# Transposes of a head issued by turns with the values of the head ahead of it, and the next stage's first weights handled ahead of a layer norm

## The chip, the cores and the metric

One core of one Trainium2 chip. The metric is the device time of one execution in microseconds (us); the kernel before has a median of 1176.0 us over three runs (1175.67 to 1176.55). Engines are called by their names or as the profile does: TensorE is PE, VectorE is DVE, ScalarE is ACT, GpSimd is POOL, SyncE is SP.

## The reference, cut to what matters

Two decoder layers over 512 positions of width 1024 in float32; each layer is a token mixer, an output projection, a layer norm, a convolutional feed-forward block and a second layer norm. The change lies in the mixer of layer 0 (16 attention heads of width 64) and at the layer norms.

```python
# layer 0: 8 heads with a learned selection of keys (a), 8 heads with a forgetting gate (b)
la = einsum('bthr,btkr->bhtk', ql, c_sel) + bias;  pa = softmax(la);  oa = einsum('bhtk,btkr->bthr', pa, c_sel)
lb = einsum('bthd,bshd->bhts', qb, k_b) + gate;    pb = softmax(lb);  ob = einsum('bhts,bshd->bthd', pb, v_b)
mix = concatenate([oa, ob]) @ w_o
x = layer_norm(ALPHA * x + mix)          # then conv_ffn and a norm; layer 1: gated MLP and short conv, norm, conv_ffn, norm
```

## The kernel before

Every product of float32 matrices is made of three reduced-precision products: both operands are split into a high and a low part, and `mms` (L183) or `mm3` (L177) issues high x high, high x low, low x high into one PSUM bank. A weight block arrives by DMA in a `raw` tile of 128 x 1024 (three of them), ACT casts the high part (L77) and DVE or POOL subtracts for the low part (L81, L79); `Stream.get` keeps two blocks split ahead of use, and a `raw` tile is free for the next load when its low part is made.

The attention of layer 0 goes head by head, 0 to 15. The 512 queries are four chunks j of 128, and causal masking leaves chunk j with 128 (j+1) keys. For a head:

- **logits** (L628): 12 products with 64-row operands, in four groups of three (128, 256, 384 and 512 columns wide), into three banks.
- **soft** (L648): for each chunk DVE adds the bias and takes the minimum (L655), and ACT takes the exponential with its sum (L657) into a tile `d`.
- **turn** (L669): ten transposes of 128 x 128 through PE (L675) bring `d` into the one `tri` area of PSUM, keys first. An odd head adds a transpose of the reciprocal sums (L678) with a small copy on ACT (L680). Then `cut2` (L227) splits all 1280 columns into `pt`: a cast on ACT (L230), then a subtraction on DVE (L231).
- **values** (L689): 12 products of `pt` with the values, 512, 384, 256 and 128 columns wide. Their stationary operand has 64 columns for an even head and 128 for an odd one. ACT copies the result out (L713).
- **divide** (L721), once for two heads: a product, a cast (L727) and a subtraction (L728).

The string `SEQ` sets in what order these are issued for the heads. It is gone through once for each h from 0 to 19: L is logits(h), B the bias of h+1, T is turn(h-1), S is soft(h), D is divide(h/2-2), V is values(h-2), and a digit is that many **fill products**, taken from the projections of later heads, which need nothing of these stages. In turn, `fill(1)` also stands after each transpose. From about head 11 on no fill products are left until the output projection's are let in at head 15. I call a stage of a head by its letter and the head's number: T11 are the transposes of head 11.

Written order is not the order that the engines get: a scheduler sorts the instructions of each engine by its own model of time, and each engine runs its list in order. So the order of each engine, and not the code alone, tells what a change moves.

A layer norm (`out_ln`, L288) works on four chunks n of 128 rows while the last products of the stage ahead run: DVE adds and takes statistics (L259 to L263), POOL raises to -0.5 (L264), DVE and ACT scale (L267, L270), POOL adds (L271), and PE transposes the chunk into the next stage's operand (L282, 4 at a time, two halves of a chunk). In its loop it lets one weight block be split ahead with each chunk: `ws.ready(base[0] + n + 1)`. There are four norms; the second one (between the feed-forward of layer 0 and layer 1) is the place called "the second norm" below. The first weight blocks of layer 1 are two held in `quad` tiles and then blocks in `whi`/`wlo` tiles. One block of layer 1 passes a mask on POOL ahead of its split (`mask_w`, an affine select, L817).

Of the kernel before, what the change touches and what calls it, by code (L numbers as in the profile page):

```python
# [18 lines left out]
NCH = 4  # L19
# [6 lines left out]
EPS = 1e-5  # L26
BIG = 1e30
TAIL = 4
SEQ = "L4BT2SDV3"
POOL_CUT = range(12, 23)  # L30
S1, S2, S3, S4 = 4, 3, 1, 2
WARM, WARM2 = 7, 5
# [63 lines left out]
def _body(ctx, tc, A):  # L96
# [23 lines left out]
    def quad(dt=FR):  # L120
        return quads.tile([128, 4, 512], dt, name="quad")

    ws = Stream(nc, A["ws"], rawp, wp, 2)
# [65 lines left out]
    def both(*runs):  # L189

        runs = list(runs)
        while runs:
            for r in list(runs):
                if next(r, "end") == "end":
                    runs.remove(r)

    def xk(xt, k, a=0, b=S):
        return xt[0][k // 4][:, k % 4, a:b], xt[1][k // 4][:, k % 4, a:b]
# [39 lines left out]
    def load_gb(l, i):  # L238
        q = quad(F32)
        for s, src in enumerate((A["ln_g"], A["ln_b"])):  # L240
            nc.gpsimd.dma_start(q[:, 2 * s:2 * s + 2].rearrange("p a b -> p (a b)"),
                                src[l, i].partition_broadcast(128))
        return [q[:, j] for j in range(4)]
# [44 lines left out]
    def out_ln(lhs, nk, res_src, l, i, dst, nbig, last=False, begun=None):  # L288

        head = nk - TAIL  # L290
        if begun is None:
            pb = [[None, None] for _ in range(NCH)]
            for hf in range(2):
                for n in range(NCH):
                    pb[n][hf] = bank()
            for k in range(head, nk + (0 if last else nbig)):
                ws.big[base[0] + k] = quad

            for k in range(head):
                w = unit()  # L300
                for hf in range(2):
                    for n in range(NCH):
                        mm3(pb[n][hf], lhs(k, n), wk(w, hf * 512, hf * 512 + 512), k == 0, False)
        else:
            pb, run = begun
            for _ in run:
                pass
        us = [unit() for _ in range(TAIL)]
        gb = load_gb(l, i)
        xt = None if last else [[quad(), quad()], [quad(), quad()]]  # L310
        rs = []
        for n in range(NCH):
            rs.append(load_res(res_src, n))
            for hf in range(2):
                for k in range(head, nk):
                    m = mm3(pb[n][hf], lhs(k, n), wk(us[k - head], hf * 512, hf * 512 + 512),
                            k == 0, k == nk - 1)
                if not last and hf == 0 and n >= 2:
                    ln_turn(n - 2, rs[n - 2], xt, m)
            ln_chunk(n, pb[n], rs[n], gb, dst)  # L320
            if not last:
                ws.ready(base[0] + n + 1)
        late = None if last else [lambda m, n=n: ln_turn(n, rs[n], xt, m) for n in (2, 3)]
        return xt, late
# [54 lines left out]
    with ExitStack() as m0:  # L379
# [248 lines left out]
        def logits(h):  # L628

            q = made[h // 2]  # L630
            d = biases.pop(h)
            r = slice(64 * (h % 2), 64 * (h % 2) + 64)
            b01, b2, b3 = bank(), bank(), bank()
            lg = [b01[:, :128], b01[:, 128:384], b2[:, :384], b3]

            def run(j):
                n = 128 * (j + 1)
                c = slice(j * 128, j * 128 + 128)
                return mms(lg[j], (q[r, 0, c], q[r, 1, c]), (q[r, 2, :n], q[r, 3, :n]), True, True)

            both(run(0), run(2))
            both(run(1), run(3))
            st_[h] = (d, lg)

        rd_d = dr.tile([8, 2 * NCH, 128], F32, name="rd_d")
# [23 lines left out]
        def turn(h):  # L669
            d = st_[h][0]  # L670
            p = tri.tile([128, 1536], F32, name="tri")
            for i in range(NCH):
                for j in range(i, NCH):
                    o = PO[i] + (j - i) * 128
                    nc.tensor.transpose(p[:, o:o + 128], d[:, OFF[j] + i * 128:OFF[j] + i * 128 + 128], ident)  # L675
                    fill(1)
            if h % 2 == 1:
                nc.tensor.transpose(p[:8, 1280:1408], rds.pop(h // 2), ident)  # L678
                row = temp()[:8, :128]
                nc.scalar.copy(row, p[:8, 1280:1408])  # L680
                nc.scalar.dma_start(rd_d[h // 2], row)
            pt = ptp.tile([128, 2, 1280], FR, name="pt")
            cut2(pt[:, 0], pt[:, 1], p[:, :1280])
            st_[h] = pt

        oq = []
# [2 lines left out]
        def values(h):  # L689
            pt = st_.pop(h)  # L690
            if h % 4 == 0:
                oq.append(quad())
            i = h // 2
            v = vB if h < 8 else vA
            b0 = 64 * (h % 2)
            r = slice(b0, b0 + 64)
            p = bank()
            m = b0 + 64
            hv = h % 8
            if h % 2 == 0:  # L700
                ot[i] = [temp()]
            t = ot[i][0]

            def run(k):
                f = slice(64 * hv - b0, 64 * hv + 64)
                c = slice(PO[k], PO[k] + 512 - 128 * k)
                return mms(p[:m, k * 128:], (v[0][:, k, f], v[1][:, k, f]), (pt[:, 0, c], pt[:, 1, c]),
                           k == 0, k == 2)

            both(run(0), run(3))  # L710
            both(run(1))
            both(run(2))
            nc.scalar.copy(t[r], p[r])  # L713
            if h % 2 == 1:
                rb = temp()
                for e in range(2):
                    nc.sync.dma_start(rb[64 * e:64 * e + 64], rd_d[i, 4 * e:4 * e + 4].rearrange(
                        "a b -> (a b)").partition_broadcast(64))
                ot[i].append(rb)
# [48 lines left out]
        for h in range(20):  # L768
            for c in SEQ:
                if c == "L" and h < 16:  # L770
                    while h // 2 not in finished and next(todo, "end") != "end":
                        pass
                    logits(h)
                    if h == 15:
                        for _ in todo:
                            pass
                        todo = begun
                elif c == "B":
                    bias(h + 1)
                elif c == "D" and h >= 4 and h % 2 == 0:  # L780
                    divide(h // 2 - 2)
                elif c == "S" and h < 16:
                    soft(h)
                    step(S3)
                    soft2(h)
                    step(S4)
                elif c == "T" and 1 <= h <= 16:
                    turn(h - 1)
                elif c == "V" and 2 <= h <= 17:
                    values(h - 2)  # L790
                elif c.isdigit():
                    fill(int(c))
        ps3.close()
# [185 lines left out]
```

## Time and profile before

| | |
|---|---|
| median of three runs | 1176.0 us (1175.67 to 1176.55) |
| the profiled execution, its own time | 1176.91 us |
| its span on the core | 1175.2 us, of 14440 instructions |
| mean granted clock of PE | 0.995 of full speed |
| PE busy | 1160.9 us, 99% |
| DVE, ACT, POOL busy | 59%, 40%, 16% |

The span is the profiler's window on the core, 1.7 us shorter than the time of the same execution. The heads from 11 on, which have no fill products between their stages, lie at 194 to 222 us; the second norm lies at 620 to 650 us. A busy PE is a PE that has work; whether that work is at full clock is told by the granted clock of the stretch (1.00 is the 2.4 GHz level, 0.50 the 1.2 GHz level).

### The profile page before, as it was taken

What the parts mean: (1) busy time and instruction counts of PE and PEld (TensorE: products, weight loads), DVE (VectorE), ACT (ScalarE), POOL (GpSimd) and SP (SyncE); (2) the same over time, 40 slices, a digit from 0 to 9 for tenths busy, and PEclk for the clock granted to TensorE, in tenths of its full rate; (3) what the DMA queues carried; (4) which work ended last, traced back from release to release, by engine and by line L of the source; (5) the groups of instructions that cost most, each with busy time, mean ns of one, the idle gap of its engine ahead of it and who ended that gap; (6) DMA issues with size and microseconds to landing.
All of it is one profiled execution on the core that took longest, in us unless ns stands there. A gap on an engine that the chain in (4) does not pass through costs nothing. (4 is left out here: it accounts for less than half of the span.)

```text
span 1175.2 us, 14440 instructions
## 1 busy us (share of the span) xinstructions
PE 1160.9 (99%) x5532; PEld 967.0 (82%) x5532; DVE 697.9 (59%) x1137; ACT 464.5 (40%) x701; POOL 185.5 (16%) x242
## 2 busy tenths in 40 slices
PE   9999999999999999999999999999999999999997
PEld 7887878789888888888888888889888888888885
DVE  6799975657656666552237854465665565652226
ACT  7625656623444443432234243332544434432121
POOL 1319645314000000010004200012000000010003
PEclk9999999899999999999999999999999999999999
DMA  7623202353232322343353234371223223344221
GB/s 245 228 73 103 60 32 69 99 161 126 76 104 90 106 92 92 124 141 127 108 164 112 75 108 129 125 239 64 90 90 105 92 93 104 108 144 143 92 88 72
DMA packets 41381, 132.03 MB, mean 112 GB/s; under 512 B 5448, under 2 KB 5520, under 8 KB 41312
## 3 DMA queue, kind: packets, MB, share of 16 engines
q1 hardware_dynamic: 36128, 115.36, 30.3%
q0 software_dynamic: 5056, 15.71, 4.2%
q8 instruction: 43, 0.70, 0.3%
q14 instruction: 26, 0.21, 0.1%
q10 hardware_dynamic: 128, 0.03, 0.0%
HBM read 122.63 MB, written 10.02 MB: 113 GB/s over the span
## 5 line engine op out<-in xcount | busy, mean ns | idle before, releaser
L81 DVE TENSOR_TENSOR wlo<-raw,whi 128x1024 fp32r<-128x1024 f32 x150 | 185.2, 1235 | 273.1 <-ACT whi L77 272.9
L179 PE MATMUL bank<-quad,whi 128*128 128x512 f32 (+2 forms) x860 | 325.5, 380 | 0.4 <-ACT whi L144 0.4
L180 PE MATMUL bank<-quad,whi 128*128 128x512 f32 (+2 forms) x860 | 325.3, 378 | 0.0
L181 PE MATMUL bank<-quad,wlo 128*128 128x512 f32 (+2 forms) x860 | 325.2, 378 | 0.0
L77 ACT CAST whi<-raw 128x1024 fp32r<-128x1024 f32 x158 | 166.2, 1053 | 238.1 <-PE bank L181 107.3
L179 PEld LDWEIGHTS bank<-quad,whi 128*128 128x128 f32 x860 | 161.7, 188 | 31.2 <-ACT whi L144 1.5
L181 PEld LDWEIGHTS bank<-quad,wlo 128*128 128x128 f32 x860 | 161.7, 188 | 29.7
L180 PEld LDWEIGHTS bank<-quad,whi 128*128 128x128 f32 x860 | 161.7, 188 | 29.2
L180 PE MATMUL bank<-wlo,quad 128*128 128x512 f32 x356 | 138.5, 389 | 0.0
L181 PE MATMUL bank<-whi,quad 128*128 128x512 f32 x356 | 138.3, 389 | 0.0
L179 PE MATMUL bank<-whi,quad 128*128 128x512 f32 x356 | 138.0, 389 | 0.0
L249 POOL DMA_DIRECT2D temp<-x x24 | 13.2, 548 | 566.8 <-ACT quadx L365 424.4
L180 PEld LDWEIGHTS bank<-wlo,quad 128*128 128x128 f32 x356 | 66.8, 188 | 14.0
L181 PEld LDWEIGHTS bank<-whi,quad 128*128 128x128 f32 x356 | 66.8, 188 | 14.0
L179 PEld LDWEIGHTS bank<-whi,quad 128*128 128x128 f32 x356 | 66.8, 188 | 13.6
L334 DVE SCALAR_TENSOR_TENSOR temp<-bank,fcw,temp 128x511 f32<-128x511 f32 x88 | 65.5, 744 | 9.1 <-ACT temp L333 9.1
L180 PE MATMUL bank<-quad 128*128 128x512 f32 (+1 forms) x192 | 68.5, 358 | 0.6 <-DVE quad L81 0.6
L179 PE MATMUL bank<-quad 128*128 128x512 f32 (+1 forms) x192 | 67.8, 357 | 0.5 <-ACT quad L230 0.5
L181 PE MATMUL bank<-quad 128*128 128x512 f32 (+1 forms) x192 | 67.9, 356 | 0.0
L336 DVE SCALAR_TENSOR_TENSOR temp<-bank,fcw,temp 128x510 f32<-128x510 f32 x88 | 65.9, 748 | 3.0
L333 ACT ACTIVATE temp<-bank,fcw 128x512 f32<-128x512 f32 x88 | 60.0, 682 | 10.8 <-PE bank L181 10.8
L361 ACT ACTIVATE temp<-temp 128x512 f32<-128x512 f32 x44 | 27.8, 632 | 89.0 <-DVE temp L336 89.0
(164 smaller groups left out, 1479.3 us busy)
## 6 DMA issues: line engine op xcount, KB each, us to landing
raw<-in_ws_dram SPq DMA_DIRECT2D x190, 512.0 KB, 3.5
x<-temp SPq DMA_DIRECT2D x24, 256.0 KB, 2.0
temp<-x POOLq DMA_DIRECT2D x24, 256.0 KB, 3.2
temp<-in_xT_dram SPq DMA_DIRECT2D x8, 256.0 KB, 6.7
temp<-fk_d SPq DMA_DIRECT2D x8, 256.0 KB, 3.8
temp<-rd_d SPq DMA_DIRECT2D x16, 128.0 KB, 3.8
temp<-in_x_dram POOLq DMA_DIRECT2D x8, 256.0 KB, 3.5
quad<-in_ln_g_dram POOLq DMA_DIRECT2D x4, 512.0 KB, 4.9
```

Of the source, the lines that this page charges most:

```text
L77: nc.scalar.copy(hi, t)
L81: dve[0] = nc.vector.tensor_tensor(out=lo, in0=t, in1=_f(hi), op=ALU.subtract)
L179: nc.tensor.matmul(out, a[0], b[0], start=first, stop=False)
L180: nc.tensor.matmul(out, a[0], b[1], start=False, stop=False)
L181: return nc.tensor.matmul(out, a[1], b[0], start=False, stop=last)
L249: nc.gpsimd.dma_start(t, src[n * 128:n * 128 + 128, hf * 512:hf * 512 + 512])
L333: nc.scalar.mul(t, p, cw[:, j, 2:3])
L334: nc.vector.scalar_tensor_tensor(out=t[:, 1:], in0=p[:, :S - 1], scalar=cw[:, j, 1:2], in1=t[:, 1:], op0=ALU.mult, op1=ALU.add)
L336: nc.vector.scalar_tensor_tensor(out=t[:, 2:], in0=p[:, :S - 2], scalar=cw[:, j, 0:1], in1=t[:, 2:], op0=ALU.mult, op1=ALU.add)
L361: nc.scalar.activation(tg, tg, AF.Silu)
```

## The change

1. `SEQ` goes from "L4BT2SDV3" to "L7BX5SD7". X takes the products of turn(h-1) and of values(h-2) **by turns**, a transpose and then a product, until one of them is out. The fill products in T are gone; a head has 19 of them before (4 + 10 + 2 + 3) and after (7 + 5 + 7).
2. The transposes go by chunks of queries (`JS`): all that needs chunk 0 first, then chunk 1, and so on; before, they went by chunks of keys.
3. For heads 12 to 15 the split of `pt` comes in two pieces, of 512 and 768 columns.
4. In values, the products of 384 columns are no longer mixed with the rest: first 512 and 128 by turns as before, then 384, then 256 (in a generator that X can take from).
5. `out_ln` calls `ws.ready` for two blocks more than the next stage's `quad` blocks ahead of the norm's loop, when it is not the last norm.

The code from L196 on moves down by 2 to 8 lines: L230 becomes L233, L675 becomes L682, L186 becomes L187, L77 and L81 become L78 and L82.

```diff
-SEQ = "L4BT2SDV3"
+SEQ = "L7BX5SD7"
+JS = (0, 1, 2, 3)
...
         us = [unit() for _ in range(TAIL)]
         gb = load_gb(l, i)
+        if not last:
+            ws.ready(base[0] + nbig + 2)
...
-            for i in range(NCH):
-                for j in range(i, NCH):
+            for j in JS:
+                for i in range(j + 1):
                     o = PO[i] + (j - i) * 128
                     nc.tensor.transpose(p[:, o:o + 128], d[:, OFF[j] + i * 128:OFF[j] + i * 128 + 128], ident)
-                    fill(1)
+                    yield
...
-            cut2(pt[:, 0], pt[:, 1], p[:, :1280])
+            for c in ((slice(0, 1280),) if h < 12 else (slice(0, 512), slice(512, 1280))):
+                cut2(pt[:, 0, c], pt[:, 1, c], p[:, c])
...
-            both(run(0), run(3))
-            both(run(1))
-            both(run(2))
+            yield from both(run(0), run(3))
+            yield from run(1)
+            yield from run(2)
...
-                elif c == "T" and 1 <= h <= 16:
-                    turn(h - 1)
-                elif c == "V" and 2 <= h <= 17:
-                    values(h - 2)
+                elif c == "X":
+                    for _ in both(*([turn(h - 1)] if 1 <= h <= 16 else []),
+                                  *([values(h - 2)] if 2 <= h <= 17 else [])):
+                        pass
```

**The last heads on ACT.** The list of ACT in the kernel before, from the cast of head 10's `pt` (`pt_2149`) to that of head 11's (`pt_2217`); `d_2128` is head 12, and the three casts to `quad` are weight blocks of the output projection.

```order
L230 CAST pt_2149<-tri_2135 128x1280
L713 COPY temp_2092<-bank_2163 64x512
L657 ACTIVATE d_2128,den_2221<-d_2128,mn_2220 128x384
L727 CAST quad_2090<-temp_2092 128x512
L77 CAST quad_2408<-raw_2406 128x1024
L77 CAST quad_2413<-raw_2411 128x1024
L77 CAST quad_2418<-raw_2416 128x1024
L657 ACTIVATE d_2128,den_2221<-d_2128,mn_2220 128x128
L657 ACTIVATE d_2128,den_2221<-d_2128,mn_2220 128x256
L680 COPY temp_2214<-tri_2202 8x128
L230 CAST pt_2217<-tri_2202 128x1280
```

The same stretch after; `d_2131` is head 12, `d_2195` head 13, `pt_2229` is the probabilities of head 11 (those of head 10 stand 4 rows ahead of the first row).

```order
L664 ACTIVATE d_2131,den_2236<-d_2131,mn_2235 128x256
L664 ACTIVATE d_2131,den_2236<-d_2131,mn_2235 128x384
L664 ACTIVATE d_2131,den_2236<-d_2131,mn_2235 128x512
L735 CAST quad_2060<-temp_2062 128x512
L78 CAST quad_2412<-raw_2410 128x1024
L78 CAST quad_2417<-raw_2415 128x1024
L78 CAST quad_2422<-raw_2420 128x1024
L664 ACTIVATE d_2195,den_2306<-d_2195,mn_2305 128x128
L664 ACTIVATE d_2195,den_2306<-d_2195,mn_2305 128x256
L664 ACTIVATE d_2195,den_2306<-d_2195,mn_2305 128x384
L687 COPY temp_2226<-tri_2202 8x128
L233 CAST pt_2229<-tri_2202 128x1280
```

Between the cast for head 10 and that for head 11 there now stand all four exponentials of head 12 and three of head 13; before, three of head 12 and none of head 13.

**The same heads on PE.** The kernel before, from the last products of V10's first group: `bank_2235` is V10, `bank_2250` to `bank_2252` L13, `tri_2202` T11, `bank_2297` V11.

```order
L186 MATMUL bank_2235<-pt_2149,quad_1552 64x128
L186 MATMUL bank_2250<-quad_1863 128x128 x3
L186 MATMUL bank_2250<-quad_1863 128x256 x3
L675 MATMUL tri_2202<-ident_137,d_2038 128x128 x10
L678 MATMUL tri_2202<-ident_137,rd_2085 8x128
L186 MATMUL bank_2235<-pt_2149,quad_1552 64x512
```

And after, the same work; `bank_2204` is V10, `bank_2250` and `bank_2251` L13, `tri_2202` T11.

```order
L187 MATMUL bank_2204<-pt_2160,quad_1521 64x128
L187 MATMUL bank_2250<-quad_1846 128x128 x3
L187 MATMUL bank_2250<-quad_1846 128x256 x3
L187 MATMUL bank_2251<-quad_1846 128x384 x3
L682 MATMUL tri_2202<-ident_137,d_2051 128x128 x3
L187 MATMUL bank_2204<-pt_2160,quad_1521 64x512
L682 MATMUL tri_2202<-ident_137,d_2051 128x128
L187 MATMUL bank_2204<-pt_2160,quad_1521 64x128
L682 MATMUL tri_2202<-ident_137,d_2051 128x128
L187 MATMUL bank_2204<-pt_2160,quad_1522 64x512
L682 MATMUL tri_2202<-ident_137,d_2051 128x128
L187 MATMUL bank_2204<-pt_2160,quad_1522 64x128
```

The ten transposes of T11 stood in a row; now three do, and a product of V10 follows each of the rest. V11 follows in both kernels when V10 and L13 are done, and T12 is by turns with V11 in the same way.

**The second norm on DVE and POOL.** The list of DVE before: the first row is the last of the feed-forward's blocks, `wlo_5454` and `wlo_5460` are later blocks of layer 1, `temp_5214` is the norm's chunk 0.

```order
L81 TENSOR_TENSOR quad_5204<-raw_5202,quad_5204 128x1024
L81 TENSOR_TENSOR wlo_5454<-raw_5451,whi_5453 128x1024
L259 SCALAR_TENSOR_TENSOR temp_5214<-temp_5214,bank_4641 128x512
L261 BN_STATS st_5242<-temp_5214 128x6
L259 SCALAR_TENSOR_TENSOR temp_5216<-temp_5216,bank_4645 128x512
L81 TENSOR_TENSOR wlo_5460<-raw_5457,whi_5459 128x1024
L261 BN_STATS st_5242<-temp_5216 128x6
```

The first two blocks of layer 1 come some 25 rows later, in the middle of the norm's last chunk (`temp_5374`):

```order
L259 SCALAR_TENSOR_TENSOR temp_5374<-temp_5374,bank_4644 128x512
L81 TENSOR_TENSOR quad_5371<-raw_5369,quad_5371 128x1024
L81 TENSOR_TENSOR quad_5435<-raw_5433,quad_5435 128x1024
L261 BN_STATS st_5416<-temp_5374 128x6
L259 SCALAR_TENSOR_TENSOR temp_5376<-temp_5376,bank_4648 128x512
```

After, all of them stand ahead of chunk 0 (`temp_5244`), with `wlo_5740` behind its first row:

```order
L82 TENSOR_TENSOR quad_5212<-raw_5210,quad_5212 128x1024
L82 TENSOR_TENSOR quad_5220<-raw_5218,quad_5220 128x1024
L82 TENSOR_TENSOR quad_5225<-raw_5223,quad_5225 128x1024
L82 TENSOR_TENSOR wlo_5231<-raw_5228,whi_5230 128x1024
L82 TENSOR_TENSOR wlo_5237<-raw_5234,whi_5236 128x1024
L262 SCALAR_TENSOR_TENSOR temp_5244<-temp_5244,bank_4649 128x512
L82 TENSOR_TENSOR wlo_5740<-raw_5737,whi_5739 128x1024
L264 BN_STATS st_5272<-temp_5244 128x6
L262 SCALAR_TENSOR_TENSOR temp_5246<-temp_5246,bank_4653 128x512
```

On POOL, the mask stood behind three chunks of the norm; after, it stands ahead of the first chunk's power (L267, L264 before):

```order
L244 DMA quad_5215<-in_ln_b_dram 128x1024
L825 AFFINE_SELECT raw_5749<-raw_5749 128x1024
L267 TENSOR_TENSOR rs_5275<-ve_5274,mhalf_140 128x1
L274 TENSOR_TENSOR temp_5244<-temp_5244,quad_5215 128x512
L274 TENSOR_TENSOR temp_5246<-temp_5246,quad_5215 128x512
```

The two `quad` blocks and the two after them are now split in the order in which they are loaded, and the mask of a later block is on POOL ahead of the norm.

## Rows read from the trace of the kernel before

**Rows 1.** Busy time of each engine, share of the span, instructions (the page).

```profile
PE 1160.9 (99%) x5532; PEld 967.0 (82%) x5532; DVE 697.9 (59%) x1137; ACT 464.5 (40%) x701; POOL 185.5 (16%) x242
```

**Rows 2.** Stretches: length, busy time of PE, PEld, DVE, ACT, POOL; clock; DMA share, GB/s.

```profile
100.00:194.00 94.00, 94.00 (x510) 74.74 (x509) 74.42 (x189) 59.09 (x130) 59.23 (x93) 1.00 0.23 71
194.00:222.00 28.00, 26.40 (x148) 21.89 (x146) 21.15 (x54) 21.24 (x51) 14.14 (x20) 0.88 0.29 87
...
630.00:660.00 30.00, 29.40 (x144) 23.91 (x144) 27.73 (x62) 13.19 (x20) 17.09 (x15) 1.00 0.40 142
```

**Rows 3.** PE's timeline in the last heads: start, length, line, operation, [idle before <- releaser].

```profile
201.30 2.19 PE L186 MATMUL bank<-quad 64*128 64x128 f32 x12
...
209.99 0.56 PE L186 MATMUL bank<-pt,quad 128*128 128x512 f32 x2 [0.96 <-ACT pt L230]
...
213.65 2.37 PE L675 MATMUL tri<-ident,d 128*128 128x128 f32 x10 [0.63 <-DVE rd L665]
215.66 3.60 PE L186 MATMUL bank<-pt,quad 128*128 128x512 f32 x12
219.19 2.17 PE L186 MATMUL bank<-quad 64*128 64x128 f32 x12
```

**Rows 4.** Finer stretches of the last heads, columns as in rows 2.

```profile
212.00:214.00 2.00, 1.37 (x6) 0.82 (x5) 2.00 (x6) 1.32 (x5) 0.45 (x1) 0.53 0.78 236
...
218.00:220.00 2.00, 2.00 (x12) 1.73 (x12) 1.45 (x2) 0.58 (x1) 1.34 (x3) 0.77 0.00 0
```

**Rows 5.** PE's paces in the heads before: fill products, transposes and values.

```profile
156.88 0.48 PE L186 MATMUL bank<-quad 128*128 128x512 f32 x1
...
157.22 0.48 PE L186 MATMUL bank<-quad 128*128 128x512 f32 x1
...
161.21 2.07 PE L186 MATMUL bank<-pt,quad 128*128 128x512 f32 x12
163.12 0.39 PE L186 MATMUL bank<-quad,whi 128*128 128x512 f32 x1
...
180.05 1.25 PE L675 MATMUL tri<-ident,d 128*128 128x128 f32 x10
181.06 0.48 PE L186 MATMUL bank<-quad,whi 128*128 128x512 f32 x1
```

**Rows 6.** ACT's timeline in the last heads.

```profile
204.72 2.95 ACT L77 CAST quad<-raw 128x1024 fp32r<-128x1024 f32 x3
207.56 0.40 ACT L657 ACTIVATE d<-d,mn 128x128 f32<-128x128 f32 x1
...
208.73 1.21 ACT L230 CAST pt<-tri 128x1280 fp32r<-128x1280 f32 x1
```

**Rows 7.** DVE's timeline in the last heads.

```profile
201.59 1.49 DVE L231 TENSOR_TENSOR pt<-tri,pt 128x1280 fp32r<-128x1280 f32 x1 [0.42 <-ACT pt L230]
203.00 0.55 DVE L655 CUSTOM_DVE_ANT_0 d<-bank,d 128x384 f32<-128x384 f32 x1
```

**Rows 8.** The second norm: PE, ACT and POOL timelines, and the mask's line.

```profile
636.40 0.60 PE L282 MATMUL bank<-ident,temp 128*128 128x128 f32 x4
...
646.30 0.40 PE L181 MATMUL bank<-quad 128*128 128x512 f32 x1
646.53 0.39 PE L179 MATMUL bank<-quad 128*128 128x512 f32 x1
647.47 0.50 PE L180 MATMUL bank<-quad 128*128 128x512 f32 x1 [0.55 <-DVE quad L81]
...
631.50 1.05 ACT L77 CAST whi<-raw 128x1024 fp32r<-128x1024 f32 x1 [4.87 <-DMA raw<-in_ws_dram]
...
629.95 0.99 POOL L264 TENSOR_TENSOR rs<-ve,mhalf 128x1 f32<-128x1 f32 x1 [75.22 <-DVE ve L263]
633.25 2.97 POOL L271 TENSOR_TENSOR temp<-temp,quad 128x512 f32<-128x512 f32 x2 [2.31 <-ACT temp L270]
...
L817 POOL TENSOR_SCALAR_AFFINE_SELECT raw<-raw x1: 1100/1100/1100, 650.3 to 650.3; 128x1024 f32<-128x1024 f32 x1
```

More of the change, by code (lines that the diff above doesn't have):

```diff
@@ L195, in both @@
                     runs.remove(r)
+                else:
+                    yield
     def xk(xt, k, a=0, b=S):
@@ L639, in run @@
                 return mms(lg[j], (q[r, 0, c], q[r, 1, c]), (q[r, 2, :n], q[r, 3, :n]), True, True)
-            both(run(0), run(2))
-            both(run(1), run(3))
+            for _ in both(run(0), run(2)):
+                pass
+            for _ in both(run(1), run(3)):
+                pass
             st_[h] = (d, lg)
@@ L671, in turn @@
             p = tri.tile([128, 1536], F32, name="tri")
-            for i in range(NCH):
-                for j in range(i, NCH):
+            for j in JS:
+                for i in range(j + 1):
                     o = PO[i] + (j - i) * 128
                     nc.tensor.transpose(p[:, o:o + 128], d[:, OFF[j] + i * 128:OFF[j] + i * 128 + 128], ident)
-                    fill(1)
+                    yield
             if h % 2 == 1:
@@ L786, in _body @@
                     step(S4)
-                elif c == "T" and 1 <= h <= 16:
-                    turn(h - 1)
-                elif c == "V" and 2 <= h <= 17:
-                    values(h - 2)
+                elif c == "X":
+                    for _ in both(*([turn(h - 1)] if 1 <= h <= 16 else []),
+                                  *([values(h - 2)] if 2 <= h <= 17 else [])):
+                        pass
                 elif c.isdigit():
```

## The prediction

> **What bounds the kernel now.** I read the busy time of the engines first: PE is busy for 1160.9 us, 99% of the span [rows 1], so the time can only move where PE has idle time, where its clock is low, or where the same products take longer in another order. The number of PE's products of each kind is the same in both orders. Next I read the table of stretches. From 100 to 194 us, in the heads that have fill products, PE is busy for 94.00 of 94.00 us at clock 1.00; whatever those heads wait for on ACT or DVE is covered. From 194 to 222 it is busy for 26.40 of 28.00 us at a mean clock of 0.88, and from 630 to 660 for 29.40 of 30.00 [rows 2]. So there are two places to look at, the last heads and the second norm.
>
> In the last heads PE's timeline shows two waits, 0.96 us at 209.99 for the high half of head 11's probabilities and 0.63 us at 213.65, ahead of T12 [rows 3]. The second is put down to DVE's reciprocals, but T12 writes the one `tri` area, which DVE still reads for the low half of head 11, so I take it as a wait for that. After these waits the clock is at its lower level, 0.50, from about 212 to 219 [rows 4]. T12 took 213.65 to 215.66, 2.01 us, where ten transposes in a row at full clock take 1.01 [rows 3, 5]. The twelve values behind it took 3.53 us, where twelve with 128-column weights take 1.91 [rows 3, 5]. That is 1.0 + 1.6 = 2.6 us given to the clock, and with the waits the last heads lose 4.2 us.
>
> **The change part by part.**
>
> *Order of transposes and values.* Two 512-wide fill products with a transpose between them start .34 us apart (156.88 and 157.22), and without one .23 apart (646.30 and 646.53), so a transpose among wide products costs .11 us; ten in a row cost .101 each [rows 5, 8]. Where a transpose stands is therefore worth about .01 us. The 128-column weights of an odd head cost more behind narrow work; counted in the two orders there are 27 fewer places at which one 128-column operand is loaded behind another narrow product. The price of such a place is bounded by 0 and by the .101 us of a transpose in a row; I take half, .05, which gives -1.35 us. Against it stand 63 more changes from transposes to others, at .01 each (+.7), and four more entries into or exits from the 64-row logits at about .1 each, +.4. The sum is -.25, which I can't tell from nothing; bounds -2 and +1.5.
>
> *Fill products.* Nineteen for a head before and after, in other places. The 94 us without idle time say that the cover is ample [rows 2]; nothing.
>
> *The last heads.* Here nothing covers. I follow the new lists of ACT and DVE from s, the start of L12 (201.30 in the kernel before [rows 3]). The old numbers in that scale: head 11's cast at s+7.43, its end at s+8.64, V11 able to start at 209.99-.96 = 209.03, s+7.73 [rows 3, 6].
>
> On DVE the low half of head 10 (1.42 to the next start, 201.59 to 203.00 [rows 7]) now stands behind the minima of two chunks of head 12, whose products are first done about s+1; so it runs from about s+1.6 to s+3.0. The 384-wide minimum behind it takes about .5 (.55 with its tail [rows 7]), to s+3.5; the 512-wide one, by its width some .65, to s+4.2; and the product of the division, as wide, to s+4.8. Head 12's 384-wide exponential starts on ACT at s+3.55 and takes .6 by its width (.4 for 128 columns [rows 6]). ACT goes on with the 512-wide exponential (about .7), which the old list had behind head 11's cast, to s+5.0; the division's cast, .5, to s+5.5; three weight casts, 204.72 to 207.56 = 2.84 [rows 6], to s+8.3; three exponentials of head 13, some 1.5 (0.4 to 0.6 each, [rows 6]), to s+9.8; the row copy, .15; and the cast of head 11, 1.2, to s+11.1. V11 starts on PE then. PE is ready for it at about s+7.5: the same L12, V10, L13 and T11 as before stand ahead, with one return to the logits less. So the wait grows from .96 to about 3.7 us. The old wait ahead of T12 goes: head 11's low half can run at about s+11.5 to s+13, and the products of L14 stand ahead of T12 till about s+13.7.
>
> The clock fell after .96 us of idle time, so I take it that it falls after 3.7 too. The same work follows (L14, T12, V11, some of L15), and I take the same loss, 2.5 us; bounds 0 (it doesn't fall) and 3.4 (half of the 6.8 us at the lower level, if every product in it was stretched). Behind L15 the products of the output projection cover the rest in both kernels, and the split of `pt` in two pieces has nothing to win there: it is two more instructions on each of ACT and DVE for four heads, under that cover. Sum of the last heads: 3.7 + 2.5 = 6.2 against 4.2, **+2.0 us**.
>
> The Trainium skill (TensorE: Matmul & The Clock Gate, Part 4, PE-mode transpose) says that transposes do not count as PE being busy for the clock. In this trace the clock came back in the stretch 218 to 220, during values and logits and not during T12 [rows 4], which agrees but decides nothing. By that rule T12 spread over V11 would keep the clock low for longer, by at most those ten transposes at half clock and the products between them, some 1.7 us; it is the last rival below.
>
> *The second norm.* PE waits for the low halves of the two `quad` blocks, which DVE makes only then (the wait of .55 [rows 8]). The product at 647.47 would have started at 646.76 by the pace of .23, so .7 us are lost, and I add .2 for the block ahead, whose low half is made just before; the stretch has .60 in all by its busy time [rows 2], which is the lower bound. Both blocks are now split ahead of the norm, so **-.9 us**. What is late next: the norm's first transposes, which stood behind 11 more products before (636.40 less 11 x .227, so due at 633.9) [rows 8]. Their chain in the old trace is: power on POOL at 629.95, a cast on ACT at 631.50 that waited for its load and held the scaling up, POOL's additions from 633.25 to 636.2 [rows 8]. In the new order the casts are done before, and the scaling can follow the power at 631; but the mask, 1.1 us on POOL [rows 8], must be through before the power, and its block's load, three loads behind the `quad` blocks, has to land by about 629. I get the first addition done at 633.3 and the second at 634.8, against due times of 633.9 and 634.8. No wait, with nothing to spare.
>
> *Sum.* -.25 + 2.0 - .9 = +.85. The profiled execution took 1176.91 us, .9 above the median of the runs, and its losses are taken to be those of a median run; 1176.0 + .85 = **1176.9 us**.
>
> **The rivals.** A run can be told from no change at about 0.2%, 2.4 us.
>
> 1. *The wait comes but the clock holds*: 3.7 against 4.2 in the last heads, with the norm and the order -1.65: **1174.3**. For it: an idle time that starts a little later or breaks in two might pass; against it: the clock fell after a quarter of that idle time [rows 3, 4].
> 2. *The wait does not come* (faster). If ACT's exponentials of head 13 and the casts are through earlier than I add up, by more than 3 us, the wait is under .6, the clock stays, and all 4.2 us of the last heads are won: 1176.0 - 4.2 - .9 - .25 = **1170.7**. For it: V11's wait of .96 turned into a loss of 4.2, so little decides much. Against it: the order of ACT's list, in which 2.5 us of work have moved ahead of head 11's cast.
> 3. *Transposes by turns cost what 64-row products cost* (slower). Entering or leaving the logits costs about .1 us; if each change between transposes and values did so, 63 more groups have 126 more changes, up to +11 us: **1183 to 1188**. For it: no transposes stand between values in the old trace. Against it: between fill products they cost only .11 [rows 5, 8]. It decides from .03 us a change on.
> 4. *The mask is late* (slower). POOL's list is held until the block has landed; the loads took some 4 to 5 us each while ACT waited for them (4.87 [rows 8]), and a load that lands 2 us late moves the power, the norm and PE's wait by 2: **1179.5**, decided from some .5 us on.
> 5. *The clock stays low for longer in T12 and V11*: 1176.9 + 1.7 = **1178.6**.
>
> **How the numbers follow.** My forecast has .42; rival 1 has .14, rival 2 .18, rival 3 .07, rival 4 .13, rival 5 .06. The forecast, rival 1 and a part of rival 5 are within 0.2% (1173.6 to 1178.4), less the edges: .52 for the same. Faster: rival 2 and the lower edge of rival 1, .26. Slower: rivals 3, 4, the rest of 5 and the forecast's upper edge, .22. The range takes in rival 2 and rival 4 and leaves out rival 3 and the far ends: 1170.5 to 1180.5. The likeliest case alone has 1175 to 1178.8 (clock loss 0.6 to 3.4, order +-1).
>
> **What would show it.** In the profile after: a PE wait of 3 to 4 us for ACT's cast (L233) at about 209, a low clock for some 6 us behind it, no wait ahead of T12; no PE wait for DVE's low halves near 645, and the norm's first transposes (L285) without idle time ahead of them. I am wrong if the wait for the cast is under 1 us, if ten transposes by turns with values take more than the sum of both by over .5 us, or if PE waits for POOL at the second norm.

## The result, and the profile after

The changed kernel takes 1183.22 us by the median of 8 runs (1181.84 to 1188.55), the kernel before 1177.05 in the 8 runs beside it (1175.67 to 1180.96): ratio 1.0052, 95% interval 1.0034 to 1.007, some 6 us slower. The forecast of 1176.9 and its range up to 1180.5 are both missed.

In all kernels here PE waits early, between 52 and 57 us, in lists that are the same for every engine in all of them up to the first logits. In some profiles this takes 1 to 2 us, and the first logits start at 90.8 to 93.6 us; in the others it takes 3.8 to 4.0, with a low clock around it, and they start at 95.0 to 96.5. This moves a whole execution by up to some 4 us. So I compare profiles from the first logits on, by the starts of rows of PE's timeline: the first logits, those of head 12 (L12) and head 15 (L15), the last transpose of the first and second norm, the last product of the kernel. Each profile is of one execution; where the median of several says something else than the profile, it is said below.

| us | first logits to L12 | to L15 | to the first norm | to the second norm | to the end | sum |
|---|---|---|---|---|---|---|
| before | 109.82 | 17.89 | 71.38 | 365.29 | 510.88 | 1075.27 |
| changed | 110.33 | 21.54 | 74.83 | 364.06 | 510.88 | 1081.64 |
| difference | +0.51 | +3.65 | +3.45 | -1.23 | 0.00 | +6.37 |
| forecast | -0.25 | +2.0 | 0 | -0.9 | 0 | +0.85 |

Of the changed kernel, PE's timeline with these rows and the waits in them (the last transpose of a norm starts 0.76 us behind its row of eight; the start of L12 in the kernel before is in [rows 3]):

```profile
91.19 1.48 PE L187 MATMUL bank<-quad 64*128 64x128 f32 x8
...
201.52 2.18 PE L187 MATMUL bank<-quad 64*128 64x128 f32 x12
...
208.81 0.73 PE L187 MATMUL bank<-quad 64*128 64x512 f32 x2
212.96 0.90 PE L187 MATMUL bank<-pt,quad 128*128 128x512 f32 x2 [3.42 <-ACT pt L233]
213.78 3.89 PE L187 MATMUL bank<-quad 64*128 64x128 f32 x12
...
223.06 2.19 PE L187 MATMUL bank<-quad 64*128 64x128 f32 x12
...
232.64 0.50 PE L187 MATMUL bank<-pt,quad 128*128 128x512 f32 x1 [0.36 <-ACT pt L233]
...
250.40 0.27 PE L682 MATMUL tri<-ident,d 128*128 128x128 f32 x1
...
253.70 0.40 PE L187 MATMUL bank<-pt,quad 128*128 128x512 f32 x1
254.71 0.61 PE L187 MATMUL bank<-pt,quad 128*128 128x128 f32 x2 [0.61 <-ACT pt L233]
255.70 1.59 PE L187 MATMUL bank<-pt,quad 128*128 128x128 f32 x9 [0.39 <-DVE pt L234]
257.97 0.50 PE L187 MATMUL bank<-whi,quad 128*128 128x512 f32 x1 [0.67 <-ACT temp L721]
...
297.13 1.04 PE L285 MATMUL bank<-ident,temp 128*128 128x128 f32 x8
...
661.19 1.03 PE L285 MATMUL bank<-ident,temp 128*128 128x128 f32 x8
...
1172.83 0.39 PE L182 MATMUL bank<-quad,quadx 128*128 128x512 f32 x1
```

The wait ahead of V11 is 3.42 us, where the kernel before had 0.96 and, ahead of T12, 0.63 [rows 3]. That ahead of T12 is gone. New are the waits at V13 (232.64) and around V15, the last head: 0.61 and 0.39 for the two halves of its probabilities, and 0.67 behind it for ACT's copy of its result. A wait of 0.32 at V12, ahead of L15, is new too. The second norm has none. The row at 250.40 is the last transpose of T15, that at 253.70 the first product of V15; the same two in the kernel before lie further apart:

```profile
238.57 1.25 PE L675 MATMUL tri<-ident,d 128*128 128x128 f32 x10
...
247.12 2.08 PE L186 MATMUL bank<-pt,quad 128*128 128x512 f32 x12
```

The stretches of the changed kernel, columns as in [rows 2]:

```profile
194.00:230.00 36.00, 32.26 (x169) 25.47 (x166) 23.56 (x60) 25.31 (x60) 17.02 (x25) 0.86 0.30 89
230.00:296.00 66.00, 63.87 (x360) 54.37 (x359) 39.30 (x57) 21.79 (x33) 17.91 (x18) 1.00 0.41 136
...
636.00:666.00 30.00, 30.00 (x150) 25.00 (x149) 27.10 (x75) 11.07 (x18) 16.12 (x15) 1.00 0.26 91
```

And finer, around the wait: the clock falls while PE is idle and comes back ten microseconds later.

```profile
210.00:212.00 2.00, 0.00 (x0) 0.00 (x0) 2.00 (x4) 1.98 (x9) 2.00 (x2) 0.90 0.71 221
212.00:214.00 2.00, 1.04 (x3) 0.72 (x4) 1.96 (x2) 2.00 (x4) 2.00 (x3) 0.50 0.64 174
...
220.00:222.00 2.00, 2.00 (x11) 1.77 (x11) 0.00 (x0) 0.00 (x0) 0.00 (x0) 0.54 0.00 0
```

ACT of the changed kernel, first in the last heads, then at the split for V15:

```profile
207.09 2.93 ACT L78 CAST quad<-raw 128x1024 fp32r<-128x1024 f32 x3
209.93 0.40 ACT L664 ACTIVATE d<-d,mn 128x128 f32<-128x128 f32 x1
...
211.69 1.21 ACT L233 CAST pt<-tri 128x1280 fp32r<-128x1280 f32 x1
...
252.02 0.57 ACT L233 CAST pt<-tri 128x512 fp32r<-128x512 f32 x1
252.50 0.57 ACT L721 COPY temp<-bank 64x512 f32<-64x512 f32 x1
253.86 0.80 ACT L233 CAST pt<-tri 128x768 fp32r<-128x768 f32 x1 [0.79 <-DVE pt L234]
```

Head 11's cast starts at s+10.17, where the forecast's chain had s+9.9. The last row shows something that the forecast had not considered: the second piece's cast waits for DVE's subtraction of the first.

### The profile page after: what moved, and what is told of

It reads as the page before. It is cut to its first block, busy times and chain, and to the rows that moved or that the text cites. A ratio compares the mean times of both kernels' runs of the same rounds, so it can differ in the third digit from the quotient of the medians.

```text
span 1181.3 us, 14442 instructions
## 1 busy us (share of the span) xinstructions
PE 1163.5 (98%) x5532; PEld 967.5 (82%) x5532; DVE 697.7 (59%) x1141; ACT 465.9 (39%) x705; POOL 184.3 (16%) x242
## 5 line engine op out<-in xcount | busy, mean ns | idle before, releaser
L82 DVE TENSOR_TENSOR wlo<-raw,whi 128x1024 fp32r<-128x1024 f32 x150 | 186.2, 1242 | 270.6 <-ACT whi L78 267.8
L78 ACT CAST whi<-raw 128x1024 fp32r<-128x1024 f32 x158 | 166.2, 1053 | 227.9 <-PE bank L182 109.7
L187 PE MATMUL bank<-quad 128*128 128x512 f32 (+4 forms) x288 | 63.9, 361 | 0.0
```

The source lines that it names most:

```text
L78: nc.scalar.copy(hi, t)
L82: dve[0] = nc.vector.tensor_tensor(out=lo, in0=t, in1=_f(hi), op=ALU.subtract)
L187: nc.tensor.matmul(out, u, v, start=first and i == 0, stop=last and i == 2)
```

## The experiments

"Sum" is the time from the first logits to the end in the profile of the run (1075.27 before, 1081.64 changed). Medians stand beside that of the kernel before on the same chip.

**e1.** The weight casts of the output projection (blocks 26 to 29) are kept behind head 11's cast by an order edge.

```diff
-        nc.scalar.copy(hi, t)
+        c = nc.scalar.copy(hi, t)
+        if i in hold[1] and hold[0] is not None:
+            self.tc.add_manual_dep(c.ins, hold[0].ins.name, AFTER, reason="behind the split of a head")
...
+            if h == 11:
+                hold[0] = last_cut[0]
```

> The changed kernel, but the three weight casts of the output projection wait on ACT for the cast of head 11's probabilities. Theory (ACT's list ahead of that cast makes PE's wait, and the wait makes the clock fall): the wait of 3.4 us ahead of V11 shrinks by the casts' 2.8 to about 0.6; if the clock then holds, 2.8 + 4.4 = 7 us are won against the changed kernel (about 1176), and if it still falls, 2.8 to 5 (about 1179). Rival (transposes by turns with values make PE slower by themselves): no more than 1 us is won.

```profile
211.07 0.56 PE L192 MATMUL bank<-pt,quad 128*128 128x512 f32 x2 [0.81 <-ACT pt L240]
```

The wait went from 3.42 to 0.81 us; the clock still fell, for 3.4 us instead of 10.2. The last heads took 16.46 us instead of 21.54, the sum is 1076.83 (-4.81). ACT's list makes the wait, as held. By the median the gain is far smaller: 1182.52 against 1177.27, 1.0037 (1.0023 to 1.0051), so 5.25 us behind the kernel before, where the changed kernel was 6.17 behind. The profiled execution, 1179.08, is the second fastest of its runs; what the others lost is not shown.

**e2, e5, e6.** Work of no use is put ahead of V11, into V11's own bank: 12 transposes of the identity, 32 of them, or 15 products of 512 columns.

```diff
+            if h == 11:
+                for _ in range(12):      # e5: 32
+                    nc.tensor.transpose(p[:, :128], ident, ident)
             yield from both(run(0), run(3))
...
+                for _ in range(15):      # e6
+                    nc.tensor.matmul(p, v[0][:, 0, :128], v[0][:, 1], start=True, stop=True)
```

> The changed kernel with twelve more transposes of the identity ahead of V11, whose result is overwritten; with them the scheduler also takes L14 ahead of V11, so that PE has work through the whole wait. ACT's list is the same. Theory (idle time makes the clock fall): the clock stays at its upper level, V11 starts when it did, L14 costs nothing, 2 + 4.4 us are won against the changed kernel (about 1176.5). Rival (transposes do not keep the clock up, or the clock falls for another reason): the clock falls as before and only L14's 2 us are won, about 1181.

> The changed kernel with 32 more transposes of the identity ahead of V11, 3.5 us of them in a row (overwritten later); L14 comes between them and V11. One question: what keeps the clock up. If a row of transposes counts as work, the granted clock is 1.00 through them, and falls, if at all, only behind the next wait. If transposes do not count (the rule of rival 5), the clock falls during them or just behind them as it did in the idle time of the changed kernel, which began to be at 0.50 about 2.7 us after the last product.

> As the run with 32 transposes, but with 15 products of 512 columns in their place, 3.4 us. By either theory the clock stays at 1.00 through them; a fall here would say that neither idle time nor transposes decide.

In e2 the clock stayed at 1.00 to 222 us, but the wait moved to the next place:

```profile
221.82 0.52 PE L682 MATMUL tri<-ident,d 128*128 128x128 f32 x3 [2.91 <-DVE rd L672]
```

I take T12's wait of 2.91 us as one for the `tri` area, which DVE read until just before it. The clock fell behind that for 3.4 us, and the sum is 1079.49 (-2.15): near the rival's figure, for a reason that neither side had named. Median 1185.43 against 1177.27, 1.0061 (1.0039 to 1.0082), no better than the changed kernel's; the profiled execution has the early wait in its long form (3.89 us). In e5 PE worked through the stretch; its timeline and two stretches of it:

```profile
209.35 3.71 PE L720 MATMUL bank<-ident 128*128 128x128 f32 x32
212.99 2.17 PE L187 MATMUL bank<-quad 64*128 64x128 f32 x12
...
216.38 0.52 PE L682 MATMUL tri<-ident,d 128*128 128x128 f32 x3 [0.72 <-DVE pt L234]
```

```profile
210.00:212.00 2.00, 2.00 (x21) 2.00 (x19) 2.00 (x4) 1.98 (x8) 2.00 (x2) 1.00 0.67 242
212.00:214.00 2.00, 2.00 (x17) 1.83 (x16) 0.79 (x1) 1.99 (x4) 2.00 (x3) 1.00 0.71 201
```

The clock never fell in these heads; sum 1077.87 (-3.77), one run, 1179.25. Nothing useful was done in those 3.7 us, so what it won is the clock and L14, which now stands ahead of V11. (The expectation has the clock of the changed kernel falling 2.7 us after PE's last product; that product ended at 209.54 and the clock was down from 211.6, so it was 2.1.) In e6 the clock held through the products and fell for 3.4 us behind a wait of 1.28 at T12; sum 1081.11, one run, 1186.37.

**e3.** Without the early split ahead of the norms (the two lines `if not last: ws.ready(base[0] + nbig + 2)`).

> The changed kernel without the early split of the next stage's first blocks. Theory: the second norm loses the 0.9 to 1.2 us that it had won, about 1184.4; the other norms show nothing. Rival (the early split costs elsewhere, by the mask or the loads): 1183 or less.

The stretch to the second norm is 365.34 instead of 364.06, 1.28 us more where 0.9 to 1.2 was expected; the sum is 1082.41. Median 1188.12 against 1177.27, 1.0088 (1.007 to 1.0106), 4.9 us above the changed kernel's, which is more than this accounts for. In the profiled execution, the fastest of the six, the first logits come 2.4 us later than in the changed kernel's; the rest is not explained. PE's order up to the second norm is that of the changed kernel, yet the clock was low for 6.8 us and not 10.2, and the last heads took 20.61: so much does one order vary.

**e4.** More fill products ahead of V15.

```diff
-                    fill(int(c))
+                    fill(int(c) + (10 if h == 17 and c == "7" else 0) - (5 if h == 16 and c == "7" else 0))
```

> The changed kernel with ten fill products more ahead of V15, taken from those that stood ahead of T14 and T15 (20 instead of 12 stand between T15 and V15). Theory (too little work between T15 and V15): of the 2.7 us of waits around V15 those for the halves of its probabilities go, 1.3 to 1.9 us, about 1181.5; the wait for its bank of 0.8 stays. Rival (these waits are hidden behind something later): no change.

The waits for V15's halves are gone, the one behind it (0.67) is left, and the stretch to the first norm fell from 74.83 to 73.87, by 0.96 where 1.3 to 1.9 was expected. The second norm took it back (365.60 instead of 364.06):

```profile
640.57 0.66 PE L285 MATMUL bank<-ident,temp 128*128 128x128 f32 x4 [0.53 <-POOL temp L274]
```

There the mask on POOL waited for its block until 636.37, and the norm's power behind it. Sum 1082.27 (+0.63), so in all nothing was won; median 1183.42 against 1177.27, 1.0057 (1.0034 to 1.008).

**e7.** The edge of e1 in the kernel before.

> The kernel before, with the three weight casts of the output projection behind the cast of head 11's probabilities on ACT, and nothing else of the change. Theory (a wait of under 1 us for that cast was enough to bring the clock down): head 11's cast comes up to 2.8 us earlier, the waits of 0.96 and 0.63 go, the clock stays up: 4 us less between the start of L12 and that of L15 (17.9 before), and 1173 in all. Rival (the clock falls because transposes and logits are too little work, not for the wait): the waits go, the clock falls all the same, 1.5 us.

```profile
216.87 0.50 PE L191 MATMUL bank<-pt,quad 128*64 128x512 f32 x2 [2.54 <-ACT pt L237]
```

A miss. Both waits went and the last heads took 16.45 us, but V12 then waited 2.54 us, the clock fell at 218.5 for 6.8 us, and the next stretch took 75.89 instead of 71.38. Sum 1078.66 (+3.39); median 1179.80 against 1179.24, 1.0024 (1.0006 to 1.0042). Work taken from ahead of one cast stands ahead of the next.

**e8, e9, e10, e11.** e8 is the changed kernel with the edits of e1 and e4. e9 is the changed kernel with the split in one piece (`for c in (slice(0, 1280),)`), e10 the kernel before with the two pieces alone, e11 is e8 with one piece.

> The changed kernel with both mends: the three casts behind head 11's, and ten fill products more ahead of V15. If the two places are all that is wrong with it, the two gains add: 5 us at the last heads and 1 us at V15, so some 1177 by the median, level with the kernel before. Rival (by turns is slower by itself): it stays 2 us or more behind.

> The changed kernel with the split of the probabilities in one piece for all heads. Theory: with two pieces PE's list takes one product of V12, V13, V14 and V15 as soon as the first piece should be cast, and waits for it 0.3 to 0.9 us each time; in one piece these single products stand later and the waits at V12 to V14 go, 1 to 1.5 us between the start of L15 and the last transpose of the first norm (74.8 us in the changed kernel, 71.4 before). Rival (the waits are for ACT's work and not for where the products stand): no change there.

> The kernel before with the two pieces alone. The same theory: one product each of V12 to V14 is drawn ahead and waits, 0.5 to 1.5 us more in the stretch from L15 to the first norm (71.4 before). Rival: no change, or a gain of up to 0.5.

> The changed kernel with three mends: the weight casts behind head 11's, one piece, and ten fill products moved ahead of V15 (24 stand between T15 and V15). If these three are what was wrong, the last heads take 16.5 us (17.9 before), the stretch to the first norm 71.5 to 72.5, the second norm wins 0 to 1.2: from the first logits to the end 1073.5 to 1075.5 (1075.3 before, 1081.6 changed), level with the kernel before or up to 2 us ahead. Rival (by turns costs by itself): 1077 or more.

e8: sum 1076.10, with 16.52 to L15 and 73.83 to the first norm; the two gains add. Median 1180.78 against 1179.24, 1.0017 (1.0003 to 1.0032), by which it stays 1.5 to 2 us behind, between the theory and the rival. e9 went against what was expected: 79.80 to the first norm instead of 74.83, sum 1087.70 (one run, 1189.43):

```profile
223.67 0.50 PE L187 MATMUL bank<-pt,quad 128*64 128x512 f32 x2 [0.77 <-ACT pt L233]
...
258.29 1.82 PE L187 MATMUL bank<-pt,quad 128*128 128x512 f32 x10 [0.49 <-DVE pt L234]
```

The waits at V12 and V13 are 0.77 and 0.55, longer than with two pieces (0.32 and 0.36), and the clock fell twice more (at 226 and 291 us, 3.4 us each), the second time behind a wait of 1.82 us for DVE inside the first norm, which the changed kernel does not have. So with the turns the pieces help, by this one execution and by e11 beside e8. e11: 17.17 and 74.72, sum 1077.20, the rival's side; median 1182.70 against 1177.57, 1.0038 (1.002 to 1.0057). e10, without the turns: 72.79 to the first norm, 1.41 more than before, at the upper end of what was expected; sum 1075.91 (one run, 1177.81). Of the 1.41, 0.77 is idle time of PE, where the kernel before has none in this stretch: the 0.67 behind V15, for ACT's copy of its result, and short ones. The rest lies in products that start further apart, 0.27 of it in the 256-wide ones of the projection, and in one product of V12 that now stands behind the start of L15.

**e12.** The kernel before with the early split alone.

> The kernel before with the early split ahead of the norms alone. Theory: the second norm's stretch goes from 365.3 to 364.1 us, or stays if the mask's block lands late; nothing else moves: 1 us at best, which the median of some ten runs can hardly show. Rival (the split costs elsewhere): slower by more than that.

The second norm's stretch is 364.31 (365.29 before), the sum 1073.87, of which 0.41 is a difference in the last heads at the same order. Median 1176.47 against 1177.57, 0.9989 (0.9973 to 1.0005): the best of all kernels run, and not told from no change.

**e13, e14, e15, e16.** Fewer turns: the transposes first and then the values, from the 14th round on (e13), the same with the edits of e1 and e4 (e14), in all rounds (e15), and in all rounds with one piece (e16).

```diff
-                    for _ in both(*([turn(h - 1)] if 1 <= h <= 16 else []),
-                                  *([values(h - 2)] if 2 <= h <= 17 else [])):
-                        pass
+                    ts = [turn(h - 1)] if 1 <= h <= 16 else []
+                    vs = [values(h - 2)] if 2 <= h <= 17 else []
+                    for r in ([ts + vs] if h < 14 else [ts, vs]):      # e15, e16: h < 0
+                        for _ in both(*r):
+                            pass
```

> The changed kernel, but from the 14th round on (T13 with V12, T14 with V13, T15 with V14) the transposes come first and then the values, as before. Theory: by turns, the last transpose ends with the values and not ahead of them, so that the cast for the next head has lost the 1.2 to 1.9 us of values that hid it; with the old order there the stretch from L15 to the first norm goes from 74.8 to 72 or 72.8 (71.4 before, 72.8 with two pieces in the kernel before). The last heads up to L15 stay at 21.5, give or take the clock's 1 us. Rival (the fill products' places make the waits): the stretch stays above 74.

> The same, with the weight casts behind head 11's and the ten fill products ahead of V15. If the causes found are all: 110.3 to L12, 16.5 to L15, 72 to 72.8 to the first norm, 364.1 to 365.3 to the second: 1074 to 1076 from the first logits to the end, level with the kernel before (1075.3). Rival: a wait moves on once more and 2 us stay.

> The changed kernel with transposes first and then values in all rounds, the new places of the fill products and all else kept. It tells the new SEQ from the turns: ACT's list now has the three casts ahead of head 11's, all of head 12's exponentials, but none of head 13's. Theory: the wait ahead of V11 falls from 3.4 by the three exponentials' 1.5 and what T11 ends earlier, to about 1.5 to 2; the clock falls still; last heads 19 to 20; the stretch to the first norm 72 to 73. In all 1077 to 1079. Rival (the turns are not the cause of the drain's waits): the stretch stays above 74.

> The changed kernel without the turns and without the two pieces: what is left of it are the fill products' new places, the order of the transposes by chunks, the order in values and the early split. If the account by parts holds (the turns cost 6.2 us in all, the two pieces 1.4 in the stretch from L15 to the first norm, the early split wins up to 1.2 at the second norm), that stretch takes 71.4 us, the last heads 17.9, the second norm's 364.1 to 365.3: 1074 to 1075.3 from the first logits to the end, by the median 0 to 1.3 us ahead of the kernel before. Rival (without two pieces the drain gets longer, as it did with the turns): 1077 or more.

| us | to L12 | to L15 | to the first norm | to the second norm | sum | median or run, kernel before beside it |
|---|---|---|---|---|---|---|
| e13 | 110.33 | 21.59 | 73.69 | 364.83 | 1081.33 | 1182.72 (one run), 1177.00 |
| e14 | 110.33 | 16.33 | 72.76 | 365.00 | 1075.30 | 1179.93, 1177.00: 1.0010 (0.9995 to 1.0025) |
| e15 | 109.79 | 17.85 | 72.76 | 364.12 | 1075.40 | 1176.64 (one run), 1177.00 |
| e16 | 109.79 | 18.06 | 71.41 | 364.80 | 1074.95 | 1180.32, 1177.85: 1.0015 (1.0001 to 1.0029) |

e13 won 1.14 us of the 2.07 that e15 won in the stretch to the first norm, less than was expected of it (72 to 72.8). e14 reached the kernel before. e15 shows the whole: with the turns alone taken out of the code, 6.24 of the 6.37 us are back, in one execution. Its row of V11:

```profile
209.74 0.61 PE L187 MATMUL bank<-pt,quad 128*128 128x512 f32 x2 [1.43 <-ACT pt L233]
```

The expectation for e15 was too dark by 1 to 2 us in the last heads. e16 fits the account by parts in every stretch. Its median lies above that of the kernel before, with a sum that does not; its profile has the early wait in its longer form:

```profile
56.44 7.36 PE L481 MATMUL bank<-quad 128*128 128x384 f32 x20 [4.04 <-DVE quad L234]
```

Of its twelve executions nine took 1179.4 us or more, at mean clocks of 0.992 to 0.994, and six of the seventeen of the kernel before beside it; so the longer form seems commoner in its runs, and why it is, in lists that are the same up to there, stays open.

## Why the prediction was wrong

- **The wait ahead of V11** was right: 3.7 us forecast, 3.42 measured, by the list of ACT that was named. Without the weight casts it is 0.81 (e1), but these stood there before too; what the change adds to the list is exponentials, and e15, with three of them fewer ahead of that cast, has 1.43.
- **The clock behind it** was mis-sized. The term was 2.5 us, bounded by 3.4 from the 6.8 us of the kernel before. It was low for 10.2 us, from 211.6 to 221.8, with PE at work from 212.96 (the stretches above), so about half of 8.9 us, 4.4, was lost. The last heads cost 3.65 more instead of 2.0: 2.15 by waits (3.42 and V12's 0.32, for 0.96 and 0.63), 1.8 by the clock (4.4 for 2.6), less 0.3 elsewhere. The term is not a constant of the order: with the same order of PE up to L15, the changed kernel, e4 and e13 had 10.2 us and e3 had 6.8.
- **"Behind L15 the products of the output projection cover the rest in both kernels"** is the step that failed: nothing was forecast and 3.45 us came. I had looked at whether products were left, not at how many stand between the last transpose of a head and the first value of the same head. Before, ten products of values and 26 of the projection stood between T15 and V15; by turns, three and 12, for by turns the last transposes end with the values instead of ahead of them. Idle time of PE is 2.13 of the 3.45, where the kernel before has none in this stretch. The other 1.3 is not waiting: by the starts of their rows, transposes and values take 0.8 us longer (with one product of V12 more, which now stands behind the start of L15), and the projection's products 0.4, for which I have no cause. e15 gives 2.07 of the 3.45 to the turns, and the two pieces are the rest (72.76 to 71.41 from e15 to e16; 1.41 in e10). That the pieces have "nothing to win there" was wrong with the turns (e9) and too kind without them.
- **The order of transposes and values**: forecast -0.25, measured +0.51 up to L12, within the stated bounds (-2 to +1.5). It repeats to 0.01: 110.33 in every run with the turns, 109.79 in both without. Rival 3's price, 0.1 us for each change, is thereby excluded: it gives 11 us for 126 changes, and 0.54 us came up to L12 for 92 changes more than in e15. The time that it gave, 1183, was the time measured, by another mechanism.
- **The second norm**: -0.9 forecast, -1.23 measured (e3: 1.28 by itself). "With nothing to spare" was right too: in e1, e4, e13, e14 and e16 PE waited 0.5 us or more for POOL there, and the gain shrank or went, as rival 4 describes at a smaller size.
- **Rival 5**, that the clock stays low for longer in T12 and V11, had .06, and its effect came: the clock was low through both, up to 221.8, for 3.4 us more than in the kernel before. The 1.7 us that it gave is most of what the clock term was short of. Its reason, that transposes do not keep the clock up, is not borne out: e5 has 32 in a row at a clock of 1.00 and no fall in those heads, and in e1 the clock was back at 216.5 us, in the middle of T12 by turns with V11 (from 214.08 on). The Trainium skill (TensorE: Matmul & The Clock Gate, Part 4, PE-mode transpose) says that they do not count as PE being busy in the same way; here the measurements speak against it, for transposes of float32 and with one execution each. Why the clock stayed low for longer is open.
- **The fill products' new places** cost little by themselves: e16, with them, has the stretches of the kernel before up to the first norm within 0.2 us.

What stays open, besides, is why the clock fell behind 0.81 us of waiting in e1 and not behind 0.81 and 1.69 in e14, and why the medians of e1, e3 and e16 lie above what their profiles give.

## What to carry to other kernels

A transpose taken by turns with other work ends as late as that work, and what waits for the last transpose has lost the work that covered it: count what stands between the producer's last instruction and the consumer's first, in the list that each engine really gets, for every head and above all for the last one. Where PE is full at nearly every place, a cast moved out of one head's way stands in the next one's (e7). And compare such kernels stretch by stretch between fixed rows of the trace: stretches in which PE neither waits nor loses its clock repeat to hundredths (110.33 up to L12 in all twelve profiles with the turns), others vary by up to 0.9 us at the same order of PE, and whole executions scatter by 4.

## What was not expected of the hardware

The granted clock of one and the same order was low for 10.2 us in one execution and 6.8 in another (changed kernel, e3), worth 0.9 us in the last heads. The second of two casts out of one PSUM tile waited for DVE's subtraction of the first (0.79 at 253.86), though the two work on other columns, so two pieces did not give two engines a pipeline. What it waits for is a semaphore that DVE raises, an order that the program asks for; that the chip needs it is not shown.
